# Seven products of sums for pairs of outputs in two FFNs and an MLP, on one Trainium2 core

## The chip, the core and the metric

The program runs on one core of one Trainium2 chip as a single launch. The metric is device time in microseconds (us); lower is better. The three timed runs of the kernel before took 3346.64, 3347.20 and 3348.45 us, median 3347.2.

## The reference

Three residual blocks run one after the other on a sequence of 512 tokens with 1024 features, all in float32. Each block mixes along the sequence in its own way and ends with a feed-forward part. The change concerns these feed-forward parts:

```python
def swiglu(u, w_gate, w_up, w_down):                       # first block, twice; hidden width 2816
    return (jax.nn.silu(u @ w_gate) * (u @ w_up)) @ w_down

h2 = rmsnorm(x, ffn_norm_g)                                # second block; hidden width 2816
gate, up = jnp.split(h2 @ w_ffn_in, 2, axis=-1)
return x + (jax.nn.silu(gate) * up) @ w_ffn_out

h2 = rms_norm(x, norm_mlp_g[i])                            # third block; hidden width 4096
x = x + jnp.square(jax.nn.relu(h2 @ w_mlp_up[i])) @ w_mlp_down[i]
```

The first block has two such FFNs, ahead of and behind its mixers. "Both later FFNs" are the second one of the first block and the one of the second block.

## The kernel before, in words

**Layout.** Features lie on the 128 partitions and tokens along the free dimension, so an activation is 8 tiles of 128 x 512 (`KD` = 8). TensorE multiplies in the float32r format. To keep float32 precision every operand is a pair: `hi`, the value rounded to float32r, and `lo`, the value minus `hi`. A product of two pairs is three matmuls, hi·hi, hi·lo and lo·hi.

**A gemm.** `gemm` (L730) makes one output tile, 128 features x 512 tokens: `wcols` loads the weights of the column (1024 x 128, 512 KB) by one DMA into a raw tile (ring of 3), ACT casts it to `whi`, DVE subtracts to get `wlo` (rings of 6), and `gemm_w` (L742) issues 8 x 3 = 24 matmuls of 512 columns into one PSUM tile of tag `mm`. A PSUM tile is a whole bank (512 float32 per partition) and there are four of that tag. Then the caller's `evac` reads the bank. `gemm_halves` (L734) does the same for a few outputs in two halves of 256 tokens, so that TensorE can begin before the second half of its input is there; each half has a bank of its own.

**A feed-forward part.** `swiglu` (L1001) goes through the 22 hidden tiles in three parts of 8, 7 and 7: first gate and up of each hidden tile ("up stretch"), silu and product into the pair tiles `mids`, then 8 down gemms over the part. The first `HG` = 4 outputs run in halves, the rest through `gemm`. The MLP of `block3` does the same with four parts of 8 hidden tiles, one gemm each, with relu and square.

**The order of work.** Nothing is issued where it stands in the code. Every operation is recorded (`record`, L322) with its dependences and a price (`price`, L379), and `order` (L438) plays all operations through a model of the engines: at each moment an engine that is free takes the ready operation with the lowest number, where weights are moved ahead by `WOFF` = 4000, evacuations by `EOFF` = 4500. `emit` (L598) issues the operations in the order of time of that model; L605 is therefore the line of all instructions in the profile. The framework underneath puts in the semaphores. `VA.__getitem__` keeps track of which quarters of a tile a slice touches, for tiles in SBUF alone (L180): a PSUM tile counts as one region. In the model a float32r matmul of n columns costs max(n, 256)/2.4 + 2.67 ns, and a result of TensorE can be read 200 ns after its end.

**Other functions named below.** `outer` (L756) opens the first FFN with loads of three column blocks at a time; `gemm_tm` (L800) makes token-major outputs from loads of 256 x 512 weights; `rstd` (L820) reads one PSUM tile with ACT (`tile`, named rr) and with DVE (`tmp`, named rt).

Of the kernel before, what the change touches and what calls it, by code (L numbers as in the profile page):

```python
# [19 lines left out]
P = 128  # L20
# [102 lines left out]
]  # L123


def prep(inp):
    i = {k: np.asarray(v) for k, v in inp.items()}
    out = {}
    out["xT"] = np.ascontiguousarray(i["x"][0].T)
    out["pv"] = np.ascontiguousarray(np.concatenate([_cols(f(i)) for _, f in PV], axis=1))  # L130
    gd = np.repeat(i["gdn_dt_bias_2"].reshape(4), 4)
    ga = np.repeat(i["gdn_a_log_2"].reshape(4), 4)
    db = np.tile(i["dt_bias_3"].reshape(32), 4)
    al = np.tile(i["a_log_3"].reshape(32), 4)
    out["cr"] = np.ascontiguousarray(np.broadcast_to(np.concatenate([gd, ga, db, al, np.zeros(224, np.float32)])[None], (P, NCR)))
    for n in W_NAMES:
        w = i[n]
        if n.endswith(("_2", "_3")):
            w = w[0]
        out[n] = np.ascontiguousarray(w)  # L140
# [12 lines left out]
    ws = i["w_spatial_3"][0]  # L153
    out["wsT"] = np.ascontiguousarray(ws.transpose(2, 0, 1))
    out["bsp"] = np.ascontiguousarray(np.broadcast_to(i["b_spatial_3"][0].reshape(1, -1), (P, 8 * P)))
    out["vng"] = np.ascontiguousarray(np.broadcast_to(i["v_norm_g_3"].reshape(1, -1), (P, D)))
    out["vnb"] = np.ascontiguousarray(np.broadcast_to(i["v_norm_b_3"].reshape(1, -1), (P, D)))
    out["cst"], out["m8"], out["rst"] = _consts()
    return out


class VA:
# [100 lines left out]
class Op:  # L263
# [52 lines left out]
class Program:  # L316
# [62 lines left out]
    def price(s, o, name, first, ins, outs, pos, kw):  # L379
# [30 lines left out]
                    o.cost += 60  # L410
        else:
            v = first if isinstance(first, VA) else ins[0]
            o.cost = max(v.cols * 4 * v.shape[0] / 360.0, 450)
            o.lat = 2100

    def claim(s):

# [20 lines left out]
    def order(s):  # L438
# [60 lines left out]
        while done < len(ops):  # L499
# [20 lines left out]
            while again:  # L520
                again = False
                for e in engs:
# [56 lines left out]
                    vis = end + (o.lat if e == "DMA" else 0)  # L579
                    heapq.heappush(fin, (vis, o.i))  # L580
                    heapq.heappush(events, vis)
                    for q in o.succ:
                        so = ops[q]
                        so.t0 = max(so.t0, end + (o.lat if e == "DMA" else LAT.get((e, so.eng), 130)))
# [23 lines left out]
class K(Program):  # L608
    switch = 800

    def __init__(s, nc, tc, I, O, ctx):
# [5 lines left out]
        s.sb = ctx.enter_context(tc.tile_pool(name="sb", bufs=1))  # L617
        s.pp = ctx.enter_context(tc.tile_pool(name="pp", bufs=1, space=bass.MemoryType.PSUM))
        s.WB, s.WR = 6, 3
        s.nconst = 0  # L620
        s.pvt = s.const(NPV)
        s.ident = s.const(P)
# [88 lines left out]
    def wload(s, src, kk, mw):  # L711
        n = kk * mw
        with s.pri(-WOFF):
            raw = s.tile(D, F32, "wraw", s.WR, "wraw")[:, :n]
            hi = s.tile(D, F32R, "whi", s.WB, "whi")[:, :n]
            lo = s.tile(D, F32R, "wlo", s.WB, "wlo")[:, :n]
            s.D.dma_start(raw.rearrange("p (k m) -> p k m", m=mw), src)
            s.A.copy(hi, raw)
            s.V.tensor_tensor(lo, raw, hi.bitcast(F32), ALU.subtract)
        return hi.rearrange("p (k m) -> p k m", m=mw), lo.rearrange("p (k m) -> p k m", m=mw)  # L720

    def wcols(s, nk, w, c0, mw, row0):
        ws = []
        for k0 in range(0, nk, 8):
            kk = min(8, nk - k0)
            src = w[row0 + k0 * P:row0 + (k0 + kk) * P, c0:c0 + mw].rearrange("(k p) m -> p k m", p=P)
            ws.append(s.wload(src, kk, mw))
        return ws

# [26 lines left out]
    def outer(s, mats):  # L756
# [7 lines left out]
        def load(q):  # L764
            for w, c0, n in mats:
                raw = s.c("w0")[:, :n * P]
                hi, lo = s.c("w0p", dt=F32R)[:, :n * P], s.c("w0p", dt=F32R)[:, :n * P]
                s.D.dma_start(raw, w[q * P:(q + 1) * P, c0:c0 + n * P])
# [9 lines left out]
            s.big = False  # L778
        return load, mult, pss

    def gemm_f32(s, xs, specs, halves=False):


        ws = []
        for w, c0, _, row0 in specs:
            with s.pri(-WOFF):
                raw = s.tile(D, F32, "wraw", s.WR, "wraw").rearrange("p (k m) -> p k m", m=P)
                s.D.dma_start(raw, w[row0:row0 + D, c0:c0 + P].rearrange("(k p) m -> p k m", p=P))
# [11 lines left out]
    def gemm_tm(s, xs, w, c0, evac):  # L800
# [2 lines left out]
        pss = [s.ps("mm") for _ in range(NT)]  # L803
        s.big = True
        for k0 in range(0, nk, 2):
            wh, wl = s.wload(w[k0 * P:(k0 + 2) * P, c0:c0 + T].rearrange("(k p) m -> p k m", p=P), 2, T)
# [191 lines left out]
        k.V.scalar_tensor_tensor(acc[:, sh:], src[:, :T - sh], wcols[sh], acc[:, sh:], ALU.mult, ALU.add)  # L998


def swiglu(k, us, wg, g0, wu, u0, wd, down, done=()):  # L1001

    parts = ((0, 8), (8, 15), (15, 22))
    for pi, (a, b) in enumerate(parts):
        last = pi == len(parts) - 1
        mids, tmp = {}, {}

        def evs(cc):
            def ev_g(ps, sl):
# [4 lines left out]
            def ev_u(ps, sl):  # L1014
                t = tmp[cc][:, sl]
                k.V.tensor_tensor(t, t, ps, ALU.mult)
                mids[cc] = k.pair(t, mids.get(cc), sl)
            return ev_g, ev_u

# [26 lines left out]
def block1(k):  # L1046
# [274 lines left out]
    base3, us = modulated(ln, k.eps5, a3, b3, ga, ba)  # L1321
    g3 = gate_col(8, 0.5, "g3h")
    ln3 = LayerNorm(k, base3)

# [2 lines left out]
        if last:  # L1327
            ln3.add(m, sl)

    swiglu(k, us, I["ffn2_w_gate"], 0, I["ffn2_w_up"], 0, I["ffn2_w_down"], down2)  # L1330

    def final(sl):

# [19 lines left out]
    k.gemm_halves(xs, [(w, m * P, evs(m), 0) for m in range(KD - HT, KD)])  # L1353


def normed(k, x, R, col, out, sl):
    for q in range(KD):
        t = k.c("h")[:, sl]
# [4 lines left out]
def rms_normed(k, rm, eps, x, col):  # L1363
    hs = [k.newpair() for _ in range(KD)]
    for sl in HALVES:
        with k.pri(-EOFF):
            normed(k, x, rm.finish(D, eps, sl), col, hs, sl)
    return hs


# [397 lines left out]
def block2(k, final):  # L1768
# [75 lines left out]
    x = []  # L1844
    rm = RmsSum(k)
    residual(k, yp, I["w_out_2"], xd, x, rm)
    hs = rms_normed(k, rm, k.eps6, x, lambda q: k.pv("ffn_norm_g_2", q))
    rm2, rm3 = RmsSum(k), RmsSum(k)

    def down(last, m, ps, sl):  # L1850
# [2 lines left out]
            rm2.add(x[m], sl)  # L1853
            rm3.add(x[m], sl, col=k.pv("final_norm_g_2", m))

    swiglu(k, hs, I["w_ffn_in_2"], 0, I["w_ffn_in_2"], D_FF, I["w_ffn_out_2"], down)
# [66 lines left out]
def block3(k, xd, hs, out):  # L1923
# [193 lines left out]
    x = []  # L2117
    rm = RmsSum(k)
    residual(k, mp, I["w_out_3"], xd, x, rm)
    hs = rms_normed(k, rm, k.eps6, x, lambda q: k.pv("norm_mlp_g_3", q))  # L2120
    rm = RmsSum(k)
    NQ = 4
    for qt in range(NQ):
        mids, specs = {}, []
        for cc in range(8):
            def ev(ps, sl, cc=cc):
                t = k.c("sg")[:, sl]
                A.activation(t, ps, AF.Relu)
                V.tensor_tensor(t, t, ps, ALU.mult)
# [5 lines left out]
        for w, c0, ev, _ in specs:  # L2135
            k.gemm(hs, w, c0, ev)
        ms = [mids[cc] for cc in range(8)]

        def down(m):
# [23 lines left out]

def build(nc, arrays):
    I = {n: nc.dram_tensor(n, a.shape, mybir.dt.from_np(a.dtype), kind="ExternalInput").ap() for n, a in arrays.items()}
    out = nc.dram_tensor("outT", (D, T), F32, kind="ExternalOutput").ap()
    with TileContext(nc) as tc, ExitStack() as ctx:
        k = K(nc, tc, I, out, ctx)
# [10 lines left out]
```

## Time and profile before

| | |
|---|---|
| timed runs, median of 3 | 3347.2 us |
| profiled execution, its own time | 3346.65 us |
| its span from first to last instruction | 3344.9 us |
| granted TensorE clock, mean | 0.994 |
| TensorE (PE), matmuls | 3295.2 us busy, 99% of the span, 16723 instructions |
| TensorE, weight loads (PEld) | 2777.7 us, 83% |
| VectorE (DVE) | 2023.3 us, 60%, 3513 instructions |
| ScalarE (ACT) | 1408.3 us, 42%, 2130 instructions |
| GpSimd (POOL) | 0.2 us, 4 instructions |
| DMA | 358.58 MB, mean 107 GB/s |

Times in rows are microseconds from the start of the span unless marked ns. A row of the timeline gives start, duration, engine, operation, output<-inputs with shape, count, and in brackets how long the engine was idle before it and what ended that. Matmuls overlap: a matmul's duration holds the time through the array, so the pace is read from start to start.

### The profile page before, as it was taken

The numbers are of one execution on the slowest core, as the hardware profiler recorded it, in microseconds if no ns is written. First come the engines' busy times: TensorE is split into PE (matmuls) and PEld (weight loads), VectorE is DVE, ScalarE is ACT, GpSimd is POOL, SyncE is SP. The second block draws the span as 40 slices with busy tenths as digits, with TensorE's granted clock in tenths as the row PEclk, the third lists the DMA queues.
The fourth block names the chain that finished last, engine by engine and source line by source line (L and its number), as shares of the span: only waits on it lengthen the run. The fifth ranks groups of instructions, "written<-read, shape, count | busy, mean of one in ns | idle before, by whom it ended". The sixth has DMA issues, their size and how long they took to land.

```text
span 3344.9 us, 42406 instructions
## 1 busy us (share of the span) xinstructions
PE 3295.2 (99%) x16723; PEld 2777.7 (83%) x16723; DVE 2023.3 (60%) x3513; ACT 1408.3 (42%) x2130; POOL 0.2 (0%) x4
## 2 busy tenths in 40 slices
PE   8999999999999999999999999999999999999998
PEld 6888887889888878898788988888888888898887
DVE  7874699997533378873534633336548678564444
ACT  4222438453422255854422432235336556443222
POOL 0000000000000000000000000000000000000000
PEclk9999999999999999999999999999999999999999
DMA  9763242322433332312134333334344434433331
GB/s 303 248 214 101 59 129 79 101 83 76 120 95 96 93 99 58 89 39 64 45 95 121 100 103 96 97 88 139 98 131 117 113 102 115 136 95 98 95 101 57
DMA packets 584775, 358.58 MB, mean 107 GB/s; under 512 B 14240, under 2 KB 547376, under 8 KB 584576
## 3 DMA queue, kind: packets, MB, share of 16 engines
q1 hardware_dynamic: 584576, 355.88, 36.7%
q8 instruction: 131, 2.15, 0.3%
q14 instruction: 68, 0.56, 0.1%
HBM read 347.29 MB, written 8.53 MB: 106 GB/s over the span
## 4 chain that ended last, share of the span: by engine, by line
PE 96%; DVE 2%; DMA 1%; ACT 1%; issue 0%; SPq 0%; DVEq 0%; ACTq 0%
PE mm L605 86%; PE sm L605 8%; PE acc L605 2%; PE outer L605 1%; DMA ada<-ada_w 0%; DVE x L605 0%; ACT L605 0%; DVE rt L605 0%; DVE hb L605 0%; DVE lo L605 0%; DMA w<-ffn_w_gate 0%; DVE rmsq L605 0%; DVE xr L605 0%; ACT u L605 0%; DVE wlo L605 0%
## 5 line engine op out<-in xcount | busy, mean ns | idle before, releaser
L605 PE MATMUL mm<-hi,whi 128*128 128x512 f32 (+1 forms) x4505 | 1650.8, 369 | 12.9 <-ACT hi L605 12.6
L605 PE MATMUL mm<-lo,whi 128*128 128x512 f32 (+1 forms) x4505 | 1656.7, 369 | 2.0 <-DVE lo L605 2.0
L605 PE MATMUL mm<-hi,wlo 128*128 128x512 f32 (+1 forms) x4505 | 1657.1, 369 | 0.7 <-DVE wlo L605 0.7
L605 ACT CAST whi<-wraw 128x1024 fp32r<-128x1024 f32 (+2 forms) x544 | 556.5, 1023 | 1319.3 <-PE mm L605 977.5
L605 PEld LDWEIGHTS mm<-hi,whi 128*128 128x128 f32 x4505 | 851.0, 190 | 156.2 <-ACT hi L605 13.8
L605 DVE TENSOR_TENSOR wlo<-wraw,whi 128x1024 fp32r<-128x1024 f32 (+2 forms) x544 | 646.2, 1188 | 542.3 <-ACT whi L605 522.2
L605 PEld LDWEIGHTS mm<-lo,whi 128*128 128x128 f32 x4505 | 852.7, 189 | 142.1 <-issue 3.0
L605 PEld LDWEIGHTS mm<-hi,wlo 128*128 128x128 f32 x4505 | 852.9, 189 | 139.7 <-issue 2.3
L605 ACT ACT_TABLE_LOAD x135 | 173.2, 1283 | 21.0 <-DVE pj L605 8.1
L605 DVE TENSOR_TENSOR sg<-sg,mm 128x512 f32<-128x512 f32 (+1 forms) x103 | 66.1, 643 | 166.0 <-PE mm L605 164.2
L605 DVE SCALAR_TENSOR_TENSOR hb<-glu,k,hb 128x495 f32<-128x495 f32 (+27 forms) x240 | 161.9, 730 | 1.0 <-ACT hb L605 0.9
L605 DVE TENSOR_TENSOR xb<-xb,mm 128x512 f32<-128x512 f32 (+1 forms) x92 | 52.5, 571 | 177.1 <-PE mm L605 176.7
L605 DVE SCALAR_TENSOR_TENSOR x<-mm,k,x 128x512 f32<-128x512 f32 (+1 forms) x71 | 45.2, 637 | 88.1 <-PE mm L605 88.0
L605 DVE SCALAR_TENSOR_TENSOR adaacc<-ada,k,adaacc 128x512 f32<-128x512 f32 (+2 forms) x133 | 87.7, 665 | 5.8 <-DMA ada<-ada_w 3.3
L605 ACT CAST hi<-sg 128x512 fp32r<-128x512 f32 (+1 forms) x106 | 62.3, 588 | 46.8 <-DVE sg L605 45.5
L605 DVE TENSOR_TENSOR lo<-sg,hi 128x512 fp32r<-128x512 f32 (+1 forms) x106 | 68.5, 647 | 19.9 <-ACT hi L605 19.9
L605 PE MATMUL mm<-wlo,hi 128*128 128x512 f32 x192 | 76.7, 400 | 0.0
L605 PE MATMUL mm<-whi,hi 128*128 128x512 f32 x192 | 76.2, 397 | 0.0
L605 PE MATMUL mm<-whi,lo 128*128 128x512 f32 x192 | 75.9, 395 | 0.0
L605 ACT ACTIVATE sg<-mm 128x512 f32<-128x512 f32 (+1 forms) x103 | 57.3, 557 | 6.2 <-PE mm L605 6.1
L605 DVE TENSOR_TENSOR rmsq<-rmsq,rq 128x256 f32<-128x256 f32 (+1 forms) x82 | 38.7, 480 | 22.9 <-ACT rq L605 22.6
L605 ACT ACTIVATE rq<-xb 128x256 f32<-128x256 f32 (+1 forms) x48 | 21.7, 452 | 63.4 <-DVE xb L605 63.4
(400 smaller groups left out, 2548.1 us busy)
## 6 DMA issues: line engine op xcount, KB each, us to landing
wraw<-w_in SPq DMA_DIRECT2D x196, 512.0 KB, 3.9
ada<-ada_w SPq DMA_DIRECT2D x144, 256.0 KB, 5.0
wraw<-w_ffn_in SPq DMA_DIRECT2D x44, 512.0 KB, 3.9
wraw<-ffn_w_gate SPq DMA_DIRECT2D x41, 512.0 KB, 3.9
wraw<-ffn_w_up SPq DMA_DIRECT2D x41, 512.0 KB, 3.9
wraw<-w_mlp_up SPq DMA_DIRECT2D x32, 512.0 KB, 4.2
wraw<-w_mlp_down SPq DMA_DIRECT2D x32, 512.0 KB, 3.9
wraw<-ffn_w_down SPq DMA_DIRECT2D x32, 448.0 KB, 3.4
```

Source lines behind the costliest of these rows:

```text
L605: o.fn(*a, **kw)
```

## The change

In both later FFNs and in the MLP, outputs after the first four are made in pairs: gate and up of a hidden tile, or two neighbouring tiles of the MLP. A pair is a 2 x 2 product of blocks: two outputs, two halves of the 1024 input features, two halves of the 512 tokens. The eight block products become seven, each of a sum of weight blocks with a sum of input blocks (4 feature tiles x 3 matmuls x 256 tokens); the outputs are sums of the seven. Two consecutive products use the two halves of one PSUM tile. The sums of the inputs are made once per stage (`seven_inputs`), the sums of the weights per pair. For the three products whose weights are no sums, `lo` is made by ACT as -`hi`, to which a DMA of the POOL queue adds the weights again from DRAM. The FFNs are cut into four parts (6, 6, 5, 5). In the MLP the square is now made by ACT where the sum lies in SBUF. All weights of gemms lie in DRAM by blocks, `[column block, partition, feature tile, 128]`: a column load has 4 KB in one piece per partition instead of 8 pieces of 512 bytes; `outer` and `gemm_tm`, which read several column blocks side by side, have pieces of 512 bytes instead of 1.5 KB and 2 KB, and `gemm_tm` issues two DMAs per load instead of one. `normed` keeps the float32 values of its result in `u32` (8 tiles), which `seven_inputs` reads.

```diff
+class Weights:
+    def get(s, r0, nk, c0, n=1):
+        c = (c0 - sum(m for a, m in s.cuts if c0 >= a + m)) // P
+        if n == 1:
+            return s.ap[c, :, r0 // P:r0 // P + nk, :]
+        return s.ap[c:c + n, :, r0 // P, :].rearrange("n p m -> p n m")
...
-        if len(reg) == 4 and len(full) > 1 and not s.t.psum:
+        if len(reg) == 4 and len(full) > 1 and (not s.t.psum or s.t.name == "seven"):
...
-    "ssd_er": 2, "ssd_cb": 3, "ssd_bt": 2, "w8": 4, "w0": 6, "w0p": 12,
+    "ssd_er": 2, "ssd_cb": 3, "ssd_bt": 2, "w8": 4, "w0": 6, "w0p": 12, "wsum": 2, "st": 4, "cf": 4,
...
+    def seven_inputs(s, us, u32):
+        H = KD // 2
+        t1, t2 = HALVES
+        A, V = s.A, s.V
+        out = [[], [], [], []]
+        for q in range(H):
+            a, b = u32[q], u32[q + H]
+            f1, f2 = s.c("cf"), s.c("cf")
+            c5, c6, c3, c7 = f1[:, t1], f1[:, t2], f2[:, t1], f2[:, t2]
+            V.tensor_tensor(c5, b[:, t2], a[:, t2], ALU.subtract)
+            V.scalar_tensor_tensor(c6, c5, -1.0, a[:, t1], ALU.mult, ALU.subtract)
+            V.scalar_tensor_tensor(c3, c6, -1.0, b[:, t1], ALU.mult, ALU.subtract)
+            V.tensor_tensor(c7, a[:, t1], a[:, t2], ALU.subtract)
+            for o, f in zip(out, (c5, c6, c7, c3)):
+                p = s.c("s7", dt=F32R)
+                hi, lo = p[:, t1], p[:, t2]
+                A.copy(hi, f)
+                V.tensor_tensor(lo, f, hi.bitcast(F32), ALU.subtract)
+                o.append((hi, lo))
...
+    def seven(s, ins, specs):
...
+        def split(key, raw, src=None):
+            hi, lo = half()
+            A.copy(hi, raw)
+            if src is None:
+                V.tensor_tensor(lo, raw, hi.bitcast(F32), ALU.subtract)
+            else:
+                A.activation(lo, hi.bitcast(F32), AF.Copy, scale=-1.0)
+                s.G.dma_start(lo.rearrange("p (k m) -> p k m", m=P), src, accum_op=ALU.add)
+            ws[key] = [q.rearrange("p (k m) -> p k m", m=P) for q in (hi, lo)]
+        with s.pri(-WOFF):
+            g, u = (s.tile(D, F32, "wraw", s.WR, "wraw") for _ in range(2))
...
+            b11, b21, b12, b22 = g[:, :W], g[:, W:], u[:, :W], u[:, W:]
+            x4, x2 = s.c("wsum"), s.c("wsum")
+            split("P1", b11, w1.get(0, H, c1))
+            V.tensor_tensor(x4, b12, b22, ALU.add)
+            V.tensor_tensor(b12, b12, b11, ALU.add)
+            V.tensor_tensor(x2, b12, b22, ALU.add)
+            split("P6", x2)
+            split("P5", b12)
+            split("P2", b21, w1.get(H * P, H, c1))
+            split("P7", x4)
+            V.tensor_tensor(x2, x2, b21, ALU.add)
+            split("P4", x2)
+            split("P3", b22, w2.get(H * P, H, c2))
+        sums = [q for _ in range(4) for q in (lambda p: (p[:, t1], p[:, t2]))(s.ps("mm", "seven"))]
+        def prod(key):
+            ps = sums.pop(0)
...
+            for q in range(H):
+                xh, xl = ins[key][q]
+                s.E.matmul(ps, wh[:, q], xh, start=q == 0, stop=False, after=ps)
+                s.E.matmul(ps, wh[:, q], xl, start=False, stop=False)
+                s.E.matmul(ps, wl[:, q], xh, start=False, stop=q == H - 1)
+            return ps
...
+        p1 = prod("P1")
+        with s.pri(-EOFF):
+            A.copy(u, p1)
+        p6 = prod("P6")
+        with s.pri(-EOFF):
+            add(v, u, p6)
+        p5 = prod("P5")
+        with s.pri(-EOFF):
+            add(x, v, p5)
+        p2 = prod("P2")
+        with s.pri(-EOFF):
+            add(u, u, p2)
+            ev1(u, t1)
+        p7 = prod("P7")
+        with s.pri(-EOFF):
+            add(v, v, p7)
+            add(y, v, p5)
+        p4 = prod("P4")
+        with s.pri(-EOFF):
+            add(v, v, p4)
+            ev1(v, t2)
+            ev2(y, t2, True)
+        p3 = prod("P3")
+        with s.pri(-EOFF):
+            add(x, x, p3)
+            ev2(x, t1, True)
...
-    parts = ((0, 8), (8, 15), (15, 22))
+    parts = ((0, 8), (8, 15), (15, 22)) if u32 is None else ((0, 6), (6, 12), (12, 17), (17, 22))
...
-        for w, c0, ev, r0 in specs:
-            k.gemm(us, w, c0, ev)
+            if u32:
+                ins = k.seven_inputs(us, u32)
+        if u32:
+            for j in range(0, len(specs), 2):
+                k.seven(ins, [q[:3] for q in specs[j:j + 2]])
```

The planner also learns a POOL transfer: twice the price of a DMA, and 4 us until its data can be used.

## Rows read from the trace of the kernel before

**Rows 1.** The page, parts 1 and 2: busy time; granted clock in 40 slices.
```profile
PE 3295.2 (99%) x16723; PEld 2777.7 (83%) x16723; DVE 2023.3 (60%) x3513; ACT 1408.3 (42%) x2130; POOL 0.2 (0%) x4
...
PEclk9999999999999999999999999999999999999999
```

**Rows 2.** Busy time by window: stretch, its length, PE, PEld, DVE, ACT, POOL, clock, DMA.
```profile
861.00:1165.00 304.00, 304.00 (x1343) 251.78 (x1342) 110.06 (x121) 82.83 (x102) 0.00 (x0) 1.00 0.35 101
...
3007.00:3320.00 313.00, 313.00 (x1444) 261.90 (x1443) 127.75 (x152) 92.28 (x120) 0.00 (x0) 1.00 0.31 89
```

**Rows 3.** Timeline, PE: 55 matmuls of 256 columns, 29 of 512, first and last.
```profile
1880.00 0.28 PE L605 MATMUL mm<-hi,wlo 128*128 128x256 f32 x1
...
1886.48 0.28 PE L605 MATMUL mm<-hi,wlo 128*128 128x256 f32 x1
...
1959.64 0.39 PE L605 MATMUL mm<-hi,whi 128*128 128x512 f32 x1
...
1965.99 0.39 PE L605 MATMUL mm<-lo,whi 128*128 128x512 f32 x1
```

**Rows 4.** Waits of the whole span: who waited for whom, us, times, longest.
```profile
DVE rt L605 <- ACT rr L605: 20.0, 16, 4.5
```

**Rows 5.** Timeline, DVE and ACT: two engines reading one PSUM tile.
```profile
1895.99 0.47 ACT L605 ACTIVATE rr<-sm,k 128x256 f32<-128x256 f32 x1 [0.18 <-PE sm L605]
1896.50 0.48 DVE L605 TENSOR_SCALAR rt<-sm,k 128x256 f32<-128x256 f32 x1 [1.53 <-ACT rr L605]
...
2275.32 1.05 ACT L605 ACTIVATE rr<-sm,k 128x512 f32<-128x512 f32 x2 [1.22 <-DVE rt L605]
```

**Rows 6.** Timeline: from matmul to reader, and from DVE to a waiting matmul.
```profile
1884.68 0.28 PE L605 MATMUL mm<-hi,wlo 128*128 128x256 f32 x1
...
1885.00 0.42 DVE L605 TENSOR_TENSOR xb<-xb,mm 128x256 f32<-128x256 f32 x1 [1.55 <-PE mm L605]
...
847.59 0.41 DVE L605 TENSOR_TENSOR lo<-u,hi 128x256 fp32r<-128x256 f32 x1
...
848.06 0.39 PE L605 MATMUL mm<-lo,whi 128*128 128x256 f32 x1 [0.43 <-DVE lo L605]
848.28 0.28 PE L605 MATMUL mm<-hi,wlo 128*128 128x256 f32 x1
```

**Rows 7.** Groups by form, whole span: count, busy us, mean ns, idle before.
```profile
L605 DVE TENSOR_TENSOR x<-x,lnpiv 128x512 f32<-128x512 f32 x24 | 14.7, 685 | 2.6 <-ACT lnpiv L605 2.6
...
L605 ACT CAST hi<-sg 128x512 fp32r<-128x512 f32 x90 | 55.9, 621 | 42.5 <-DVE sg L605 41.4 <-DMA wraw<-ffn_w_down 0.3
...
L605 ACT CAST hi<-sg 128x256 fp32r<-128x256 f32 x16 | 6.4, 403 | 4.3 <-DVE sg L605 4.1
...
L605 ACT ACTIVATE sg<-mm 128x256 f32<-128x256 f32 x16 | 6.1, 383 | 6.2 <-PE mm L605 6.1
```

**Rows 8.** Timeline, DVE: eight subtractions back to back.
```profile
408.08 2.77 DVE L605 TENSOR_TENSOR lo<-u,hi 128x256 fp32r<-128x256 f32 x8
```

**Rows 9.** DMA: the queue (packets, MB, share), and issues (KB each, us to landing).
```profile
q1 hardware_dynamic: 584576, 355.88, 36.7%
...
wraw<-w_ffn_in SPq DMA_DIRECT2D x44, 512.0 KB, 3.9
...
wraw<-w_branch_gla SPq DMA_DIRECT2D x8, 256.0 KB, 2.8
```

**Rows 10.** Timeline: DVE's end of the norm, TensorE's first 512-column matmul, twice.
```profile
1923.53 0.42 DVE L605 TENSOR_TENSOR lo<-h,hi 128x256 fp32r<-128x256 f32 x1
...
1931.73 0.40 PE L605 MATMUL mm<-hi,whi 128*128 128x512 f32 x1
...
2996.56 0.76 DVE L605 TENSOR_TENSOR lo<-h,hi 128x256 fp32r<-128x256 f32 x2
...
3005.25 0.40 PE L605 MATMUL mm<-hi,whi 128*128 128x512 f32 x1
```

**Rows 11.** Busy time by window, as in rows 2, the first 40 us.
```profile
0.00:40.00 40.00, 25.64 (x97) 20.76 (x98) 24.23 (x87) 17.60 (x31) 0.20 (x4) 0.96 1.02 327
```

More of the change, by code (lines that the diff above doesn't have):

```diff
@@ L412, in price @@
             v = first if isinstance(first, VA) else ins[0]
-            o.cost = max(v.cols * 4 * v.shape[0] / 360.0, 450)
-            o.lat = 2100
+            o.cost = max(v.cols * 4 * v.shape[0] / 360.0, 450) * (2 if o.eng == "POOL" else 1)
+            o.lat = 2100 if o.eng == "DMA" else 4000
     def claim(s):
@@ L578, in order @@
                     heapq.heappush(events, end)
-                    vis = end + (o.lat if e == "DMA" else 0)
+                    vis = end + o.lat
                     heapq.heappush(fin, (vis, o.i))
@@ L583, in order @@
                         so = ops[q]
-                        so.t0 = max(so.t0, end + (o.lat if e == "DMA" else LAT.get((e, so.eng), 130)))
+                        so.t0 = max(so.t0, end + (o.lat or LAT.get((e, so.eng), 130)))
                         so.wait -= 1
@@ L716, in wload @@
             lo = s.tile(D, F32R, "wlo", s.WB, "wlo")[:, :n]
-            s.D.dma_start(raw.rearrange("p (k m) -> p k m", m=mw), src)
+            if isinstance(src, list):
+                for j, part in enumerate(src):
+                    s.D.dma_start(raw[:, j * mw:(j + 1) * mw].rearrange("p (n m) -> p n m", m=P), part)
+            else:
+                s.D.dma_start(raw.rearrange("p (k m) -> p k m", m=mw), src)
             s.A.copy(hi, raw)
@@ L767, in load @@
                 hi, lo = s.c("w0p", dt=F32R)[:, :n * P], s.c("w0p", dt=F32R)[:, :n * P]
[L768 removed]
+                s.D.dma_start(raw.rearrange("p (n m) -> p n m", m=P), w.get(q * P, 1, c0, n))
                 s.pair(raw, (hi, lo), slice(0, n * P))
@@ L779, in outer @@
         return load, mult, pss
+    def seven_inputs(s, us, u32):
[17 more added lines that the diff above has]
+                o.append((hi, lo))
+        s5, s6, s7, s3 = out
+        h = lambda x, t: (x[0][:, t], x[1][:, t])
+        return dict(P1=[h(us[q], t1) for q in range(H)], P2=[h(us[q + H], t1) for q in range(H)], P3=s3,
+                    P4=[h(us[q + H], t2) for q in range(H)], P5=s5, P6=s6, P7=s7)
@@ new lines, in seven, with half, add @@
+    def seven(s, ins, specs):
+        H = KD // 2
+        V, A = s.V, s.A
+        (w1, c1, ev1), (w2, c2, ev2) = specs
+        W = T
+        ws = {}
+        def half():
+            if not s.spare:
+                for tag, dt in (("whi", F32R), ("wlo", F32R)):
+                    t = s.tile(D, dt, tag, s.WB, tag)
+                    s.spare.append([t[:, W:], t[:, :W]])
+            r = [q.pop() for q in s.spare]
+            if not s.spare[0]:
+                s.spare = []
+            return r
+        def split(key, raw, src=None):
[3 more added lines that the diff above has]
+                V.tensor_tensor(lo, raw, hi.bitcast(F32), ALU.subtract)
+            else:
+                A.activation(lo, hi.bitcast(F32), AF.Copy, scale=-1.0)
[3 more added lines that the diff above has]
+            g, u = (s.tile(D, F32, "wraw", s.WR, "wraw") for _ in range(2))
+            s.D.dma_start(g.rearrange("p (k m) -> p k m", m=P), w1.get(0, KD, c1))
+            s.D.dma_start(u.rearrange("p (k m) -> p k m", m=P), w2.get(0, KD, c2))
+            b11, b21, b12, b22 = g[:, :W], g[:, W:], u[:, :W], u[:, W:]
[11 more added lines that the diff above has]
+            split("P3", b22, w2.get(H * P, H, c2))
+        t1, t2 = HALVES
+        sums = [q for _ in range(4) for q in (lambda p: (p[:, t1], p[:, t2]))(s.ps("mm", "seven"))]
+        def prod(key):
+            ps = sums.pop(0)
+            s.big = True
+            wh, wl = ws[key]
+            for q in range(H):
[3 more added lines that the diff above has]
+                s.E.matmul(ps, wl[:, q], xh, start=False, stop=q == H - 1)
+            s.big = False
+            return ps
+        def add(out, a, b):
+            V.tensor_tensor(out, a, b, ALU.add)
+        e1, e2 = s.c("st"), s.c("st")
+        u, v, x, y = e1[:, t1], e1[:, t2], e2[:, t1], e2[:, t2]
+        p1 = prod("P1")
[24 more added lines that the diff above has]
+            ev2(x, t1, True)
@@ L787, in gemm_f32 @@
                 raw = s.tile(D, F32, "wraw", s.WR, "wraw").rearrange("p (k m) -> p k m", m=P)
-                s.D.dma_start(raw, w[row0:row0 + D, c0:c0 + P].rearrange("(k p) m -> p k m", p=P))
+                s.D.dma_start(raw, w.get(row0, KD, c0))
             ws.append(raw)
@@ L805, in gemm_tm @@
         for k0 in range(0, nk, 2):
-            wh, wl = s.wload(w[k0 * P:(k0 + 2) * P, c0:c0 + T].rearrange("(k p) m -> p k m", p=P), 2, T)
+            wh, wl = s.wload([w.get((k0 + j) * P, 1, c0, NT) for j in range(2)], 2, T)
             for tb in range(NT):
@@ L1032, in swiglu @@
             specs = specs[HG:]
-        for w, c0, ev, r0 in specs:
-            k.gemm(us, w, c0, ev)
+            if u32:
[3 more added lines that the diff above has]
+                k.seven(ins, [q[:3] for q in specs[j:j + 2]])
+        else:
+            for w, c0, ev, r0 in specs:
+                k.gemm(us, w, c0, ev)
         ms = [mids[cc] for cc in range(a, b)]
@@ L1320, in block1 @@
     ga, ba = scaled(k.pv("ln2_g"), k.pv("ln2_b"), "r3")
-    base3, us = modulated(ln, k.eps5, a3, b3, ga, ba)
+    u32 = [k.c("u32") for _ in range(KD)]
+    base3, us = modulated(ln, k.eps5, a3, b3, ga, ba, u32)
     g3 = gate_col(8, 0.5, "g3h")
@@ L1846, in block2 @@
     residual(k, yp, I["w_out_2"], xd, x, rm)
-    hs = rms_normed(k, rm, k.eps6, x, lambda q: k.pv("ffn_norm_g_2", q))
+    u32 = [k.c("u32") for _ in range(KD)]
+    hs = rms_normed(k, rm, k.eps6, x, lambda q: k.pv("ffn_norm_g_2", q), u32)
     rm2, rm3 = RmsSum(k), RmsSum(k)
@@ L2119, in block3 @@
     residual(k, mp, I["w_out_3"], xd, x, rm)
-    hs = rms_normed(k, rm, k.eps6, x, lambda q: k.pv("norm_mlp_g_3", q))
+    u32 = [k.c("u32") for _ in range(KD)]
+    hs = rms_normed(k, rm, k.eps6, x, lambda q: k.pv("norm_mlp_g_3", q), u32)
     rm = RmsSum(k)
@@ L2134, in block3 @@
             specs = specs[HG:]
-        for w, c0, ev, _ in specs:
-            k.gemm(hs, w, c0, ev)
+            ins = k.seven_inputs(hs, u32)
+        for j in range(0, len(specs), 2):
+            k.seven(ins, [q[:3] for q in specs[j:j + 2]])
         ms = [mids[cc] for cc in range(8)]
@@ L2165, in build @@
     I = {n: nc.dram_tensor(n, a.shape, mybir.dt.from_np(a.dtype), kind="ExternalInput").ap() for n, a in arrays.items()}
+    for n, cuts in BLOCKED.items():
+        I[n] = Weights(I[n], cuts)
     out = nc.dram_tensor("outT", (D, T), F32, kind="ExternalOutput").ap()
```

53 lines of the change are left out of this document (38 added, 15 removed).

## The prediction, made before the run

> **What bounds the kernel now.** I read the page's busy shares first, then the time slices, then windows of the stages that the change touches, then single instructions. TensorE is busy 99% of the span at a granted clock of 9 tenths or more in every slice [rows 1]; in the stretches of the second FFN of block 1 and of the MLP it is at 1.00, its upper level of 2.4 GHz, and busy without a gap, while VectorE (DVE) is at 36 and 41% and ScalarE (ACT) at 27 and 29% [rows 2]. So there time is the number of matmuls times their spacing, and other work counts only where TensorE comes to wait for it. The profiled execution took 3346.65 us (span 3344.9 and 1.75 around it), 0.55 below the median; the sum starts from it. A measurement of this kernel tells 0.2% (6.7 us) from no change.
>
> **Term 1, matmuls: -43.5.** 54 pairs change: 4+6+5+5 in each FFN, 2+4+4+4 in the MLP. A pair cost 2 x 8 x 3 = 48 matmuls of 512 columns; it now costs 7 x 4 x 3 = 84 of 256. Spacing: 28 steps from 1959.64 to 1965.99, 0.2268 us each, for 512 columns; 54 steps from 1880.00 to 1886.48, 0.120 us, for 256 [rows 3]. That is 48 x 0.2268 = 10.89 us against 84 x 0.120 = 10.08, so 0.806 saved, 54 times 43.5. The eighth saved in columns is partly lost, since a matmul costs some 13 ns beside its columns (2 x 0.120 - 0.2268) and there are more of them. The Trainium skill ("TensorE: Matmul & The Clock Gate", Back-to-back issue gap) gives columns / 2.4 + 2.5 ns; by that the saving would be an estimated 64 us and the sum 3426, but the rows show 10 ns more per matmul, and they decide.
>
> **Term 2, taking turns at a PSUM bank: +124.5.** Before, every product group has a bank of its own. Now two products share one tile, which is one bank: P1 and P6, P5 and P2, P7 and P4, first half and second half. TensorE writes the second half while DVE or ACT should read the first. Does the program let them? In `rstd` ACT writes rr and DVE writes rt, both only reading one PSUM tile; neither needs the other's result. Yet DVE waits for ACT at rt 16 times, 20.0 us in all [rows 4]; rr runs 1895.99 to 1896.46 and rt starts at 1896.50; and at 2275.32 it is rr that waited for an rt [rows 5]. Two reads of the same data need no order, so what is ordered is use of the bank, in the order in which instructions were emitted. I take it that two halves of a bank are ordered too. The rule that speaks against this change is in the Trainium skill ("PSUM — Partial Sum Buffer", PSUM bank collisions raise a hardware error): two engines must be kept apart by bank, disjoint columns included. By that rule the sum is the one below; by these rows read narrowly, for equal columns alone, it is rival A.
>
> The planner emits in the order of its model, where `reg` now treats the halves as independent: the next product starts the moment the last one ends, with a matmul each 109 ns, and the reader is ready 200 ns after that end. So at least two matmuls of the next product are emitted ahead of the reader and some ten behind it: the reader waits for the former, the latter for the reader. Three turns a pair: the copy of P1 (ACT), x = v + P5 and v = v + P7 (DVE). The other sums read a bank that TensorE has left. A DVE turn, by [rows 6]: matmul start 1884.68 to reader start 1885.00, 0.32; reader 0.42; its end at 848.00 to the waiting matmul at 848.06, 0.06; together 0.80 instead of 0.12, so 0.68, and the matmul behind comes after 0.22 instead of 0.12, so 0.78. An ACT turn has 0.383 for the read [rows 7]: 0.745. A pair: 2 x 0.78 + 0.745 = 2.31 us, 54 times 124.5. Behind the waiting matmul stands all of TensorE's queue. Ends: 71 us (two turns bite, no slow restart) and 173 (the reader also stands behind half a 512-wide DVE operation, 0.30 each time); I take the middle, as the readers have the first priority in the planner.
>
> **Term 3, other engines in a pair: 0.** DVE: four sums and four subtractions 512 wide at 14.7/24 = 0.61, and 11 operations 256 wide (seven sums, two products, two subtractions) at (2.77 - 0.42)/7 = 0.335: 8.6 us [rows 7, 8]. ACT: ten 512-wide copies at 0.62 and five reads or casts at 0.38 to 0.40: 8.2 [rows 7]; in the MLP 11.4, with relu, square and cast for four halves. A pair takes 10.08 + 2.31 = 12.4 us on TensorE, so both fit, and the down gemms (8 x 15 x 0.227 = 27 us a part) hold little of either. Twelve half buffers against seven a pair let weights run ten products ahead. If the cover is gone, rival C. The three low parts per pair that now come from a POOL transfer which adds into SBUF have no like in the trace: between 2.8 us (a 256 KB load) and 7.8 (twice the 3.9 of 512 KB) [rows 9], nearest to the first by size; either is inside ten products of 1.44 us. Bound 5 us over all parts. More evacuations of the down gemms (4 parts instead of 3) are DVE work of 0.6 us under gemms of 3 us. At the end of each up stretch the last product's sum, product, cast and subtraction (0.32 + 2 x 0.42 + 0.40 + 0.42 + hand-overs, 2.2 us) are covered by 12 to 24 matmuls of the first down gemm, at least 2.7 us.
>
> **Term 4, the inputs of the first pair: +18.** `seven_inputs` puts 32 operations of 256 columns on DVE (10.7 us) at the lowest priority, and P6, the second product, needs nearly all. In the FFN of block 2, DVE's last subtraction of the norm ends at 1923.95, and TensorE is done with the halves at 1931.73; with P1 it can go on to 1933.2, 9.2 us later [rows 10]. DVE has in this time 10.7, six evacuations (2.0) and four operations for the pair's weights (2.4): 15.1, so 5.9 late. The MLP: 2997.32 to 3006.7, 16.1 against 9.4, 6.7 late. I take 6 for each of three stages; ends 5 and 35 in all.
>
> **Term 5, the layout: +1.** Column loads turn from 1024 pieces of 512 bytes into 128 of 4 KB; their 3.9 us [rows 9] was ahead of need nearly everywhere and gains little. The 16 loads of the first FFN's opening turn from 128 pieces of 1.5 KB into 384 of 512 bytes, where the transfers are full (DMA share 1.02, 327 GB/s) [rows 11]: 4096 more pieces. One costs 0.367 x 16 x 3344.9 / 584576 = 33.6 ns of an engine [rows 9], 8.6 us over 16 engines if pieces set the pace, 0 if bytes do; 327 GB/s against 290 at the mean piece says mostly bytes, so 2, less 1 for the loads that get shorter. Ends -3 and 8. The 24 loads of `gemm_tm` become 48 on SP's queue; they are ahead of need and take nothing.
>
> **Sum:** 3346.65 - 43.5 + 124.5 + 0 + 18 + 1 = 3446.7, so 3447 us. By itself this case spans 3381 to 3515.
>
> **Rivals.** *A, faster: the halves of a bank are not ordered against each other.* Term 2 falls away: 3322. For it: the waits of rr and rt show equal columns only [rows 4, 5]. Against: nothing but the bank calls for an order there. It decides from the point where a turn costs less than 43.5 - 19 = 24 us / 162 = 0.15 us. ACT at 11.4 us could then bind in the MLP, 3340 at most.
> *B, one turn a pair:* the readers come so late in the plan that two of three fall behind the next product. 41.6 instead of 124.5: 3364. For it: DVE's load of 8.6 us in a planned 9.2; against: the readers' priority.
> *C, weights bind:* two of three raw tiles serve a pair, so the next load waits until the first is used up: 3.9 for the load, four sums, a copy, a subtraction and hand-overs, 7.8 us, and up to 5.5 of other DVE work that cuts in, 13.3 against 12.4: 49 us more, 3496. It decides once more than 4.6 us cut in.
>
> **Numbers.** Forecast 0.71, A 0.14, B 0.08, C 0.07. The range, 3355 to 3515, takes in B and C and nine tenths of the forecast, and leaves A out. Faster 0.15 (A, and a little of B), same 0.04 (B's lower part), slower 0.81.
>
> **What would show it.** In an up stretch: matmuls of 256 columns 0.12 us apart, with three gaps of 0.7 to 0.9 us a pair, put down to ACT (copy of P1) and DVE (the sums); a pair of 12.4 us; TensorE's busy share of the span down by some 3 points. At the first pair of each stage, a gap of some 6 us behind P1. The prediction is wrong if the 256-column matmuls run through without gaps, if the gaps lie ahead of a product's first matmul and are for weights, or if the opening 80 us grow.

## The result and the profile after

The changed kernel takes 3440.28 us (median of four runs, 3438.75 to 3442.2) against 3347.57 for the kernel before beside it: a ratio of 1.0278, 95% interval 1.0265 to 1.0291, so 2.8% slower. The forecast was 3447, in a range from 3355 to 3515. The profiled execution has a span of 3438.6 us, 93.7 more than before.

First the page: busy time, and the DMA queues (packets, MB, share of 16 engines).

```profile
PE 3305.4 (96%) x18607; PEld 2849.5 (83%) x18607; DVE 2345.5 (68%) x4423; ACT 1667.5 (48%) x2865; POOL 140.8 (4%) x166
...
q1 hardware_dynamic: 160512, 355.88, 33.5%
q0 software_dynamic: 23328, 42.48, 7.8%
```

TensorE falls from 99 to 96% [rows 1]: 133 us of the span are now without matmuls by this count, where it was 50. Queue q0 is new: the low parts that POOL's transfers add up. Next the waits of the whole span, as in [rows 4].

```profile
PE seven L639 <- DVE st L639: 54.3, 105, 0.9
...
DVE rt L639 <- ACT rr L639: 21.2, 19, 3.1
...
PE seven L639 <- ACT st L639: 20.9, 45, 0.6
```

There are 105 + 45 = 150 waits of TensorE on readers of a shared bank, where three turns in each of 54 pairs would make 162. The pairs wait as rt waits for rr, before and after. The timeline (start, length, engine, operation, idle before and releaser) shows one turn of each kind.

```profile
970.92 0.28 PE L639 MATMUL seven<-lo,whi 128*128 128x256 f32 x1
971.24 0.42 DVE L639 TENSOR_TENSOR st<-st,seven 128x256 f32<-128x256 f32 x1 [0.65 <-PE seven L639]
...
971.71 0.39 PE L639 MATMUL seven<-hi,wlo 128*128 128x256 f32 x1 [0.51 <-DVE st L639]
...
971.94 0.28 PE L639 MATMUL seven<-hi,whi 128*128 128x256 f32 x1
...
976.97 0.28 PE L639 MATMUL seven<-s,whi 128*128 128x256 f32 x1
...
977.29 0.37 ACT L639 COPY st<-seven 128x256 f32<-128x256 f32 x1 [0.17 <-PE seven L639]
...
977.72 0.39 PE L639 MATMUL seven<-s,whi 128*128 128x256 f32 x1 [0.46 <-ACT st L639]
977.94 0.28 PE L639 MATMUL seven<-s,wlo 128*128 128x256 f32 x1
```

The steps from matmul to matmul are 0.79 and 0.23 at the DVE turn, 0.75 and 0.22 at the ACT turn, where 0.12 would do: 0.78 and 0.73 lost, against 0.78 and 0.745 forecast. The wait column says 0.51, since the modelled end of a matmul lies behind its successor's start; what a turn costs is read from the starts. A pair comes every 12.3 us in the FFNs.

The loss of a stretch below is the sum of its steps between matmuls of pairs, less 0.12 for each. Over all 54 pairs it is 125.1 us. In the FFNs' steady parts it is 2.25 a pair, three turns; in the MLP's 1.89, since only ten turns bite in four pairs (why two are missing was not followed up). The first stretches of the stages lose 9.9 (four pairs), 11.3 (four) and 9.2 (two), so 0.9, 2.3 and 5.4 beyond their turns. The longest of these waits is in the MLP, for the sums of the inputs (tile s) on DVE:

```profile
3083.62 0.58 PE L639 MATMUL seven<-s,whi 128*128 128x256 f32 x1 [1.83 <-DVE s L639]
```

The opening is where it was: the first steps that can be matched at 74 and 258 us come 0.3 us later.

Two losses were not in the forecast. One lies ahead of the first pair of block 1: busy time by window, as in [rows 2], and two rows of TensorE's timeline.

```profile
836.00:845.00 9.00, 3.70 (x26) 3.19 (x24) 9.00 (x29) 6.24 (x15) 0.00 (x0) 0.93 0.01 2
845.00:855.00 10.00, 9.88 (x62) 9.89 (x63) 9.25 (x21) 8.55 (x19) 0.00 (x0) 0.72 0.47 154
```

```profile
843.18 0.38 PE L639 MATMUL mm<-hi,whi 128*128 128x256 f32 x1 [3.87 <-ACT hi L639]
...
845.12 0.58 PE L639 MATMUL mm<-lo,whi 128*128 128x256 f32 x1 [1.55 <-DVE lo L639]
```

DVE is busy without a break, on the norm, while TensorE stands for 3.87 + 1.55 us; then the granted clock is 0.72 over ten microseconds, part of them at the lower of its levels, 1.2 GHz, instead of 2.4: from 845.5 to 850.4 us the matmuls of 256 columns start 0.21 us apart instead of 0.12. The outputs by halves take from 837.5 to 866.8 instead of from 837.4 to 859.8: 6.9 us.

The other lies at the end of block 2's FFN. TensorE waits there for the sum of squares (rmsq) that the next norm needs, before and then after:

```profile
2273.25 1.56 PE L605 MATMUL sm<-rmsq,k 128*128 128x512 f32 x4 [1.01 <-DVE rmsq L605]
```

```profile
2343.33 2.90 PE L639 MATMUL sm<-rmsq,k 128*128 128x512 f32 x4 [3.28 <-DVE rmsq L639]
```

The matmuls behind the longer wait are slower as well. Block 2 takes 34.3 us more than before, of which its pairs explain 31.2 (47.3 lost between their matmuls, 16.1 saved); 3.1 are left, and outside the pairs this is the only step of TensorE's that grew by more than 0.2 us. The kernel with the layout alone has the short waits of before, so the long one belongs to the pairs' part of the change; why it is longer was not tested.

### The profile page after: what moved, and what is told of

Its sections match the earlier page's. It is cut to its first block, busy times and chain, and to the rows that moved or that the text cites. A ratio compares the mean times of both kernels' runs of the same rounds, so it can differ in the third digit from the quotient of the medians.

```text
span 3438.6 us, 48650 instructions
## 1 busy us (share of the span) xinstructions
PE 3305.4 (96%) x18607; PEld 2849.5 (83%) x18607; DVE 2345.5 (68%) x4423; ACT 1667.5 (48%) x2865; POOL 140.8 (4%) x166
## 3 DMA queue, kind: packets, MB, share of 16 engines
q1 hardware_dynamic: 160512, 355.88, 33.5%
q0 software_dynamic: 23328, 42.48, 7.8%
## 4 chain that ended last, share of the span: by engine, by line
PE 92%; DVE 5%; DMA 1%; ACT 1%; issue 1%; SPq 0%; DVEq 0%; ACTq 0%
PE mm L639 66%; PE seven L639 16%; PE sm L639 8%; PE acc L639 2%; DVE st L639 1%; DMA ada<-ada_w 1%; ACT st L639 0%; DVE lo L639 0%; DVE wlo L639 0%; DVE x L639 0%; PE outer L639 0%; DVE s L639 0%; DMA wraw<-w_ffn_out 0%; DVE cf L639 0%; DVE wsum L639 0%
## 5 line engine op out<-in xcount | busy, mean ns | idle before, releaser
L639 PE MATMUL mm<-hi,whi 128*128 128x512 f32 (+1 forms) x3621 | 1314.7, 365 | 15.5 <-ACT hi L639 15.1
L639 PE MATMUL mm<-lo,whi 128*128 128x512 f32 (+1 forms) x3621 | 1320.8, 366 | 3.1 <-DVE lo L639 3.1
L639 PE MATMUL mm<-hi,wlo 128*128 128x512 f32 (+1 forms) x3621 | 1319.8, 365 | 0.5 <-DVE wlo L639 0.5
L639 ACT CAST whi<-wraw 128x1024 fp32r<-128x1024 f32 (+4 forms) x668 | 574.8, 867 | 1039.1 <-PE mm L639 672.7
L639 DVE TENSOR_TENSOR wlo<-wraw,whi 128x1024 fp32r<-128x1024 f32 (+4 forms) x506 | 553.6, 1095 | 327.5 <-ACT whi L639 311.6
L639 PE MATMUL seven<-s,whi 128*128 128x256 f32 x1728 | 330.6, 287 | 13.0 <-ACT st L639 9.4
L639 PEld LDWEIGHTS seven<-s,whi 128*128 128x128 f32 x1728 | 272.7, 192 | 20.9 <-ACT st L639 13.4
L639 PE MATMUL seven<-s,wlo 128*128 128x256 f32 x864 | 247.8, 287 | 11.6 <-ACT st L639 11.6
L639 PE MATMUL seven<-hi,wlo 128*128 128x256 f32 x648 | 189.4, 292 | 31.7 <-DVE st L639 31.7
L639 PE MATMUL seven<-lo,whi 128*128 128x256 f32 x648 | 185.7, 287 | 14.4 <-DVE st L639 14.4
```

The lines of the kernel that those rows point to most:

```text
L639: o.fn(*a, **kw)
```

## Experiments

The theory to be tested: the loss is the turns at a shared bank, and nothing else in the pair binds. The chief rival: the weights or another engine bind as well, so that waits would only move. The runs came in three groups, with the kernel before beside each: 3346.0 us for the first four, 3347.7 for the next three, 3346.1 for the last three. A difference between runs of two groups is uncertain by as much, some 1.7 us.

**A bank for every product.**

```
-        sums = [q for _ in range(4) for q in (lambda p: (p[:, t1], p[:, t2]))(s.ps("mm", "seven"))]
+        sums = [s.ps("mm", "seven")[:, t1] for _ in range(7)]
```

> Each of the seven products gets a PSUM bank of its own (half of it used); nothing else is edited. In the changed kernel the 256-column matmuls of the pairs lose 125 us against a steady 0.12 us spacing, some 117 of it in 150 gaps put down to ACT (copy of P1) and DVE (the sums). Theory (turns at a shared bank): these gaps go, and the time is 3440.3 - 117 = 3323 us, between 3316 and 3337, below the kernel before. Rival (the pair is bound elsewhere too, by the raw weight tiles or by ACT's 11.4 us a pair in the MLP): the gaps move to a product's first matmul or to the weights, the pair stays at 12 us or more, and the time is 3400 to 3440.

Measured: 3333.6 us, ratio to the kernel before 0.9962 (0.9947 to 0.9977). This is 106.7 below the changed kernel (106 by the two ratios), and faster than the kernel before. Two up stretches by window:

```profile
944.00:1004.00 60.00, 60.00 (x502) 60.00 (x501) 48.99 (x101) 38.96 (x79) 12.15 (x14) 1.00 0.77 170
3066.00:3106.00 40.00, 40.00 (x336) 40.00 (x335) 32.34 (x63) 34.06 (x77) 6.94 (x8) 1.00 0.75 185
```

TensorE is full, DVE at 0.8 and ACT at 0.65 to 0.85, and a steady pair takes 10.08 us (84 steps of 0.12) with a loss of 0.0: the rival is out, in the MLP too. The 10 us that the theory promised beyond this are in the first stretches, which now lose 3.4 + 4.4 + 11.7 = 19.5 us, more than the 8.6 beyond the turns above. Part of a turn had covered the wait for the inputs' sums.

**The planner counts the whole bank.**

```
-        if len(reg) == 4 and len(full) > 1 and (not s.t.psum or s.t.name == "seven"):
+        if len(reg) == 4 and len(full) > 1 and not s.t.psum:
```

> Two products still share a bank, but the planner counts the whole tile, so that in its plan the reader of the first product comes ahead of the second product in the same bank. Theory (what costs is that the plan lets TensorE into a bank whose reader has not been): the planner has the other banks' products to put between, the turns are covered, and the time is 3320 to 3340. Rival (a bank shared by two products costs its turn whatever the plan, as TensorE then waits once for the reader ahead of the second product): 150 gaps of 0.7 to 0.8 us stay, now at a product's first matmul, and the time is 3425 to 3455.

Measured: 3335.7 us, ratio 0.9967 (0.9955 to 0.9979). The banks are shared as before, yet the turns are gone: steady parts lose 0.0 to 0.11 a pair. Two up stretches by window, and the timeline at the end of a P1:

```profile
942.00:1003.00 61.00, 60.57 (x503) 60.28 (x502) 48.84 (x101) 38.50 (x79) 12.13 (x14) 1.00 0.71 167
3068.00:3110.00 42.00, 42.00 (x345) 41.69 (x344) 31.80 (x63) 32.50 (x73) 6.94 (x8) 1.00 0.70 167
```

```profile
963.83 0.28 PE L639 MATMUL seven<-hi,wlo 128*128 128x256 f32 x1
...
963.95 0.40 PE L639 MATMUL seven<-s,whi 128*128 128x256 f32 x2
...
964.19 0.28 PE L639 MATMUL seven<-s,wlo 128*128 128x256 f32 x1
...
964.25 0.36 ACT L639 COPY st<-seven 128x256 f32<-128x256 f32 x1
...
964.31 0.40 PE L639 MATMUL seven<-s,whi 128*128 128x256 f32 x2
```

P1 (inputs hi) ends, ACT copies it, and TensorE goes on every 0.12 us with a product of the sums (inputs s) in another bank: the plan puts such a product between the two that share one. So it was not the sharing that cost the time, since 104.6 us come back with the banks still shared, but the exemption, which told the plan that there was nothing to wait for.

**Two turns instead of three.**

```
+        two = lambda: (lambda p: [p[:, t1], p[:, t2]])(s.ps("mm", "seven"))
+        one = lambda: [s.ps("mm", "seven")[:, t1]]
+        sums = one() + one() + two() + two() + one()
```

> P1 and P6 get a bank each; P5 with P2 and P7 with P4 go on sharing. One turn of three is left out, the one with ACT's copy of P1 (0.75 + 0.22 instead of 2 x 0.12 us, 0.73 each, 45 seen). Theory: 33 to 39 us less, 3401 to 3408, and two gaps a pair left. Rival (gaps are not additive: with one gone the next one grows, since the reader behind it comes earlier or later): the time stays within 10 us of 3440 or falls by more than 60.

Measured: 3410.3 us, 30 less than the changed kernel and 2 outside the theory's range. Its waits:

```profile
PE seven L639 <- DVE st L639: 56.5, 105, 1.5
```

The 105 DVE turns remain, the 45 ACT turns are gone but for one, and steady parts lose 1.54 a pair, two turns (1.70 in one of them). 45 x 0.73 = 33 are saved, less 4 by which the first stretches lose more beyond their turns (12.8 against 8.6). Turns add up one by one, to within these 4 us.

**The layout alone.** All outputs by eight products again, weights by blocks, and the new prices in the planner (the calls of `seven` and `seven_inputs` and the argument `u32` are taken out).

> Weights laid out by blocks and the planner's new prices, but all outputs by eight products as before. Theory (the layout costs 0.3 us, as landmarks at 74 and 258 us moved by that much): 3346 to 3350. Rival 1 (the stall of 6.9 us on the second half of the norm in block 1, ahead of the first pair, comes from the layout's loads): 3353 to 3357. Rival 2 (shorter column loads gain somewhere, and the pairs cost that much more than the gaps show): under 3342.

Measured: 3346.6 us, ratio 1.0003 (0.9994 to 1.0013). The layout is worth nothing in time, although the queue's packets fall from 584576 [rows 9] to 158208. There is no stall ahead of the pairs' place in block 1, which so belongs to the pairs' part of the change:

```profile
836.00:845.00 9.00, 8.85 (x71) 8.54 (x70) 9.00 (x23) 7.63 (x15) 0.00 (x0) 1.00 0.51 177
```

**The inputs' sums left out**, with a bank for every product (so is it in all that follow).

```
-        for q in range(H):
+        for q in range(0):
...
-        s5, s6, s7, s3 = out
+        s5 = s6 = s7 = s3 = [h(us[q], t2) for q in range(H)]
```

> On top of the kernel with a bank for every product (3333.6 us): the 32 sums and 16 casts of the inputs in each stage are left out, and P3, P5, P6, P7 multiply the plain second halves of the first four columns, so that the output is not the reference's. In that kernel the steady pairs lose nothing against 0.12 us a matmul, and the first stretches of the three stages lose 3.4 + 4.4 + 11.7 = 19.5 us. Theory (the first pairs wait for these sums on DVE): 3314 us, between 3311 and 3318. Rival 1 (they wait for the weights' sums): 3328 to 3334. Rival 2 (the stall on the norm of block 1, some 5.5 us, comes from the inputs' sums as well): 3307 to 3310.

Measured: 3315.5 us, 18.2 less (19.7 by the two ratios to the kernel before); all three first stretches lose 0.0, as two of them show by window:

```profile
2989.00:3009.00 20.00, 20.00 (x169) 20.00 (x168) 17.93 (x34) 15.16 (x32) 0.86 (x1) 1.00 0.80 217
868.00:908.00 40.00, 40.00 (x336) 40.00 (x335) 32.43 (x67) 24.68 (x49) 6.06 (x7) 1.00 0.75 170
```

That is what `seven_inputs` costs once nothing covers it. The stall in block 1 stays (3.86 and 1.55 us), so rival 2 is out.

**Two outputs by eight products ahead of the first pair** of each stage.

```
                 ins = k.seven_inputs(us, u32)
+                for w, c0, ev, r0 in specs[:2]:
+                    k.gemm(us, w, c0, ev)
+                specs = specs[2:]
```

> On top of the kernel with a bank for every product (3333.6 us): in each of the three stages the first two outputs behind the halves come from eight products again, so that DVE has 10.9 us more before the first pair asks for the inputs' sums. Theory: the 19.5 us go, and three pairs cost 10.89 instead of 10.05: 19.5 - 3 x 0.84 = 17 less, 3316.6 us, between 3314 and 3322. Rival (the sums have the lowest priority, so the new outputs' weights and evacuations push them back by as much): 3328 to 3337.

Measured: 3323.2 us, 10.4 less (11.7 by the two ratios). That is 1.2 outside the theory's range, less than the two groups differ by. Still lost are 2.4 us in block 2, 1.2 in the MLP and 0.9 in a later part. (An expectation below says 2.9 for the MLP; that counts as lost what 16 matmuls of 512 columns, which run between those of the pair, need beyond 0.12 each.)

**The norm held back.** In block 1 the norm's outputs went through two rotating buffers; with the change all eight have tiles of their own, since `seven_inputs` reads them later.

```
+                    kw = dict(after=us[q - 2][1]) if u32 else {}
```

> On top of the kernel with a bank for every product (3333.6 us): the scaled norm of block 1 is written no further ahead than two tiles, as it was when it went through two rotating buffers. Theory (with eight tiles of its own the norm runs ahead on DVE, and the low parts of the first weights fall behind it, so TensorE runs out of first-half products): the stall of 3.9 + 1.6 us ahead of the first pair of block 1 goes: 3328 us, between 3326 and 3330. Rival (the stall comes from a late load or from the inputs' sums): 3332 to 3335.

Measured: 3342.4 us, 8.8 more than without it. Neither held. Busy time by window, and a row of TensorE's timeline from an earlier place:

```profile
836.00:845.00 9.00, 8.85 (x71) 8.54 (x70) 8.77 (x21) 5.22 (x14) 0.00 (x0) 1.00 0.18 43
...
870.00:885.00 15.00, 9.50 (x57) 7.91 (x56) 12.70 (x33) 11.18 (x27) 1.73 (x2) 0.87 0.42 70
```

```profile
722.09 1.22 PE L639 MATMUL sm<-rmsq,k 128*128 128x256 f32 x2 [6.82 <-DVE rmsq L639]
```

The stall is gone (8.85 of 9 us busy), as the theory said; but TensorE then stands at the first pairs, for 5.5 of the 15 us from 870, with DVE at 0.85 and the clock at 0.87 there, and the first stretch, with the matmuls by halves that run in it, loses 12.3 us instead of 3.4. Put in another order, DVE's work from 833 to 885 us made TensorE wait in another place.

But the edit does more than it was meant to. Its condition holds for another norm of block 1 too, the one ahead of the mixers at some 410 us, whose results have eight tiles of their own in the kernel before as well. So two norms are held back, and the two executions differ well ahead of 833 us: the wait of 6.82 us in the row above is not in the kernel with a bank for every product, and by 794 us, ahead of the norm in question, this execution is 5.1 us behind that one, of 10.2 at the end. That the earlier norm is the reason was not tested by itself, but the 8.8 us are not the price of the norm at 833 us alone.

**Both together.**

> A bank for every product, two outputs per stage by eight products ahead of the first pair (3323.2 us so far), and the norm of block 1 held to two tiles ahead, which by itself took the stall of 5.5 us away but gave back 14 at the first pairs, where they wait for the inputs' sums on a full DVE. Theory (with the 10.9 us of cover the sums are no longer late, so the gain of the stall remains): 3316 to 3321 us. Rival (DVE is full from 833 to 885 us, and what is put ahead there is late somewhere else, cover or not): 3324 to 3335.

Measured: 3332.2 us, 9.0 more than with the outputs by eight products alone. The rival's range holds it, but in part for another reason. The two profiled executions are 4.6 us apart, and all of that is there by 794 us, behind the same wait of 6.82 us as in the run above (here at 721 us). Behind it the stall of block 1 is gone, and its first stretch loses 8.0 us instead of 0.0: the gain and the loss cancel. (The "14 at the first pairs" of the expectation were 8.9 there; most of the rest was the 5.1 ahead of 794 us.)

**Four outputs by eight products ahead of the first pair** (`specs[:4]` for `specs[:2]`).

> A bank for every product, and four outputs instead of two (3323.2 us) per stage by eight products ahead of the first pair; the first part of the MLP then has no pair. What the first pairs still lose there is 2.4 us in block 2 and 2.9 in the MLP. Theory (the inputs' sums are all that is late): 5.3 less, 3 x 0.84 more, 3320.4 us, between 3318 and 3322.5. Rival (other work on DVE takes the room that is given): 3323 to 3328.

Measured: 3318.8 us, ratio 0.9916 (0.9902 to 0.9931), in the theory's range: no step between two matmuls of pairs is over 0.15 us any more. It beats both kernels, by 0.8% and by 3.5%, with 48 pairs instead of 54. The stall in block 1 is still in it:

```profile
836.00:845.00 9.00, 3.78 (x20) 3.28 (x20) 9.00 (x26) 7.70 (x17) 0.00 (x0) 0.74 0.00 0
```

**The adding transfers twice.**

```
-                s.G.dma_start(lo.rearrange("p (k m) -> p k m", m=P), src, accum_op=ALU.add)
+                for _ in range(2):
+                    s.G.dma_start(lo.rearrange("p (k m) -> p k m", m=P), src, accum_op=ALU.add)
```

> On top of the kernel with a bank for every product (3333.6 us): each of the three transfers a pair that add a weight block onto the negated high part is issued twice, so that these low parts hold the weights once too often. They land 4.7 us after issue now. Theory (the weights run some ten products of 1.44 us ahead, so that a second 4.7 us is covered): 3330 to 3338. Rival (the low parts come just in time, and 4.7 us more a transfer shows at half the pairs or more): over 3350.

Measured: 3400.9 us, 67 more, in the rival's range; the stretches of pairs lose 84 us in all instead of 19.5, so it is there. Its queues, and two up stretches by window (the last two columns are the DMA engines' share and GB/s):

```profile
q1 hardware_dynamic: 160512, 355.88, 32.8%
q0 software_dynamic: 46656, 84.96, 15.0%
```

```profile
950.00:1019.00 69.00, 62.69 (x502) 61.67 (x501) 47.96 (x100) 38.84 (x78) 25.32 (x30) 0.98 0.95 207
2041.00:2107.00 66.00, 62.33 (x501) 60.49 (x501) 48.01 (x101) 39.26 (x78) 25.85 (x30) 1.00 0.99 217
```

The 16 DMA engines are full in these stretches, at 207 to 217 GB/s, where with one transfer they stood at 0.77. Loads suffer with them: a column of `w_ffn_in` lands after 5.3 us instead of 3.6 with one transfer. So it is more than the lateness of one low part: only some 25 of the 84 us are put down to the landing of one, while the rest wait for sums, casts and readers. That the time of the DMA engines runs out is read from their share; load and lateness were doubled together, and no run parts them.

## Why the prediction came out

The mechanism was right, and the forecast is 6.7 us above the median. That it is so near is partly luck: terms 2 and 4 together were 17 us too high (142.5 against 125.1 lost between the pairs' matmuls), and waits of some 10 us that the forecast did not have made up for most of it. By its steps:

- **Term 1, matmuls, -43.5.** Steady pairs of 10.08 us instead of 10.89 make 54 x 0.806 = -43.5. Right. (The 10.05 and 0.84 in an expectation above leave out a step at the end of each stretch.) By the gap between matmuls that the Trainium skill states ("TensorE: Matmul & The Clock Gate", Back-to-back issue gap) it was an estimated 64; the steady pairs bear the rows out, not the page. (The Trainium skill gives that formula there for an isolated matmul, and says that a stream with weight loads keeps another pace.)
- **Term 2, bank turns, +124.5.** +106.7 by the kernel with a bank for every product. Size and place of a turn were right to 0.02 us. The count was not (150, and only 45 of 54 ACT turns), and of the 125.1 us lost between matmuls of pairs, turns cover 10.9 that the first pairs would have waited anyway (19.5 without turns against 8.6 beyond them). Its reading of rr and rt [rows 4, 5], that the bank is ordered and not the columns, holds: rival A is out. The rule of the Trainium skill ("PSUM — Partial Sum Buffer", PSUM bank collisions raise a hardware error) that engines are to be kept apart by bank agrees with the order seen; no run here shows what the chip does without it, since the order was kept in every one. Rival B would have shown some 54 turns.
- **Term 3, other engines, 0.** Shown for DVE, ACT and the weights as they are: rival C is out, as a steady pair loses nothing when the turns are gone. The lead given for POOL's transfers, ten products or 14.4 us, was about right: matched in order, TensorE first reads a low part of P1 17.0 us (median) after its transfer's issue in the changed kernel, and 13.5 with a bank for every product. But the prediction priced the latency of these transfers and not their load. They bring the DMA engines to 0.77 in a stretch, and doubled they cost 67 us.
- **Term 4, the inputs' sums, +18.** 18.2 by leaving them out where there are no turns. Under the turns 8.6 us of it can be seen, not the 6 us per stage that the prediction wanted to see: 0.9, 2.3 and 5.4. Terms 2 and 4 share the 10.9 us above; the prediction added them up in full.
- **Term 5, the layout, +1.** 0.6 by itself, with an interval from -2 to +4; the opening did not grow.
- **Missing:** the 3.1 us at the end of block 2, and the stall ahead of the first pair in block 1, 6.9 us with the lower clock behind it. The prediction looked for `seven_inputs` behind the first product; it didn't ask what eight tiles instead of two rotating ones allow DVE to do first. It is shown that the stall comes with the pairs (the layout alone has none), does not come from the inputs' sums, and goes when the norm is held back (by an edit that held back an earlier norm too); that the low parts of the first weights are what falls behind is read from the timeline alone, where the first of them in this place runs 11.4 us later, here before and then after:

```profile
834.87 1.22 DVE L605 TENSOR_TENSOR wlo<-wraw,whi 128x1024 fp32r<-128x1024 f32 x1
```

```profile
846.31 1.23 DVE L639 TENSOR_TENSOR wlo<-wraw,whi 128x1024 fp32r<-128x1024 f32 x1
```

The sum with measured terms: -43.5 + 125.1 (turns and inputs' sums) + 0.6 + 6.9 + 3.1 = 92.2 of 93.7. The 1.5 us left are of the size by which the kernel before differs between groups of runs.

## What to carry to other kernels

Whoever tells a planner that two things are independent must ask what below it still orders them; here one condition cost 105 us, and without it the same seven products beat the eight, by 0.3%. Two products can share a bank for next to nothing (3335.7 us against 3333.6 with a bank each) if another bank's product is put between them. Count a saving in TensorE work against the work that it hands to DVE and DMA engines, and do so stretch by stretch: a start of a stage, where DVE is full with a norm, can cost as much as a saving brings. And an edit that is to test one place must be seen to change that place alone: compare the two traces ahead of it first.

## What was not expected

- By the time that their packets took, an adding transfer costs the DMA engines about twice a plain one by the byte: 0.078 x 16 x 3438.6 us for 42.48 MB is 101 us a MB, against 0.335 x 16 x 3438.6 / 355.88 = 52 for queue q1.
- The packets of q1 fell to little more than a quarter with the layout, its share only from 36.7 [rows 9] to 33.5%: the bytes weigh more than the pieces here.
- TensorE's granted clock fell in single places where it had waited: 0.93 and 0.72 around the stall of 3.9 us in block 1, and 0.87 in the kernel with the norm held back from 870 us on, though the slices of the page all show 9 tenths. These are mixtures of its two levels, 1.2 and 2.4 GHz. A stall on the path costs its own length and the slower matmuls behind it.
